# The fourth weight sum of every pair: made by VectorE in SBUF from a piece already there, and no longer in DRAM

## The chip, the core and the metric

The kernel runs on one core of one Trainium2 chip. TensorE (PE) multiplies matrices, and loads its weights through a stage of its own that the profile shows as PEld. VectorE (DVE), ScalarE (ACT) and GpSimd (POOL) do the element-wise work. SyncE (SP) issues DMAs; ACT and POOL issue some too. Each engine works through its own instructions in order, and semaphores hold it until what it needs is there. The metric is device time in microseconds (us), the median of several runs.

## What is computed

Two layers of an encoder trunk over 512 frames of width 1024, all in f32. What matters here is that the time goes into products of the activations with large weight matrices:

```python
for i in range(DEPTH):
    h = rmsnorm(x, norm1_g[i])
    z = h @ w_in[i] + b_in[i]
    ...
    merged = jax.nn.sigmoid(gm) * (y_m @ w_bm[i]) + jax.nn.sigmoid(gr) * (y_r @ w_br[i])
    x = x + merged @ w_out[i]
    h2 = rmsnorm(x, norm2_g[i])
    x = x + jnp.square(jax.nn.relu(h2 @ w_ff1[i] + b_ff1[i])) @ w_ff2[i] + b_ff2[i]
    h3 = rmsnorm(x, norm3_g[i])
    x = x + jax.nn.sigmoid(h3 @ w_pe_gate[i]) * (p[i] @ w_pe[i])
return rmsnorm(x, final_g)
```

## The kernel before

**Units.** The weights are used in an order that `unit_list` writes out: 165 units a layer, 330 in all. A "T8" unit is 1024 x 128 weights, 24 matmuls of 512 columns; "V" and "PE" units are of the same size. A "PAIR" unit is 1024 x 256 weights, computed by seven products instead of eight (Strassen's scheme in Winograd's form) of 12 matmuls of 256 columns each. There are 76 pairs.

**Each weight twice.** TensorE works on fp32r, so every weight piece is split into a high and a low half: `split` (lines 262 to 264) has ACT round it (`wh`) and DVE subtract (`wl`). Every product is then three matmuls: `wh` x high, `wh` x low, `wl` x high (lines 372 to 374 in a T8, 421 to 423 in a pair).

**The pieces of a pair.** The four blocks of a pair's weights are B11, B12, B21, B22, each 128 x 512 as stored. Seven products need seven weight operands: B11, B21, B22 and four sums, t1 = B12 + B11, t3 = B12 + B22, t2 = t1 + B22, t4 = t2 + B21 (the signs of the scheme are taken by the activations' side and by the readers of the products). They come in four pieces (`PIECE`): A = (B11, t1), B = (B21, t2), C = (B22, t3), each 128 x 1024, and D = (t4), 128 x 512.

**The sums.** They are made in DRAM while the kernel runs, a group of pairs at a time (20 groups; group g's tensors are `s{g}t1` to `s{g}t4`). Each sum takes two DMAs on POOL's queue (`step`, line 302): a copy of one block, then an accumulating copy of the other. `sum_steps` lists them: the first four steps of the next group alternate with the last four of this one. `due` gives the unit at which step k is issued, and `step` lets it wait for the last matmul emitted before that unit. There are 160 steps: steps 76 to 79, say, are t2 (copy of t1) of group 9, t1 of group 10, t2 (+= B22) of group 9, t3 of group 10.

**The weight feed.** `prep_next` prepares pieces in order: it lets `fill_raws` request loads ahead on SP's queue into the raw buffers `wr` (four, and a fifth, `wrx`, in the first part of a layer), then splits the next piece. A pair's A, B and C are two loads of 256 KB each, D is one. Split pieces lie in three buffers for A, B, C and T8 pieces, and one for D's. `ready` with `READY` says how far ahead of each product the pieces are prepared: before P7 of a pair, B of the next one.

**The order of a pair's products** (`run_pair`): P1, P5, then the P4 that the pair before had put off (`flush`), then P6, P2, P3, P7; its own P4 is put off in turn. P1, P6, P7 and P4 accumulate in one PSUM bank (suffix a), P5 and P3 in a second (c), P2 in a third (b). After each product, what stands in the bank is read (`done`): by DVE at L1209 or L1211 in the feed-forward pairs (`l0o10` is layer 0, block 1, pair 0), by ACT or DVE in the others (`pair_tiles`: L449 reads P2, L453 P3, L455 P7). The next product of the same bank may not begin before that.

**Other names in the steps.** `l1bgm` are the first gate tiles of layer 1, spilled to DRAM by ACT (`gm_spill`); `l1m0s` and `l1m0p` are the scores of the first mLSTM head and their weighted form (L648); `l?r0brk`, `l?r?o0` and `l?r?o1` are pairs of the retention heads; L542 is a POOL addition of the normalisation.

Of the kernel before, what the change touches and what calls it, by code (L numbers as in the profile page):

```python
# [38 lines left out]
OP = mybir.AluOpType  # L39
# [6 lines left out]
D = 1024  # L46
# [4 lines left out]
Q = 512  # L51
# [26 lines left out]
def ff_order():  # L78

    seq = [("f", 0, p) for p in range(4)]  # L80
    for b in range(3):
        seq.append(("f", b + 1, 0))
        seq += [("o", b, p) for p in range(4)]
        seq += [("f", b + 1, p) for p in range(1, 4)]
    return seq, [("o", 3, p) for p in range(4)]
# [3 lines left out]
PRODUCTS = {"P1": ("A", 0, 0), "P5": ("A", 1, 4), "P2": ("B", 0, 2), "P6": ("B", 1, 5), "P3": ("C", 0, 6),  # L89
            "P7": ("C", 1, 3), "P4": ("D", 0, 1)}  # L90

PIECE = {"A": ("B11", "t1"), "B": ("B21", "t2"), "C": ("B22", "t3"), "D": ("t4",)}

GIVEN = ("B11", "B12", "B21", "B22")
MADE = {"t1": ("B12", "B11"), "t3": ("B12", "B22"), "t2": ("t1", "B22"), "t4": ("t2", "B21")}

READY = {"P1": 2, "P4": 2, "P5": 3, "P2": 4, "P6": 4, "P3": 4, "P7": 5}


def due(k):  # L100

    return 3 + 5 * min(k, 20) // 4 + 7 * max(k - 20, 0) // 4


def groups():
# [108 lines left out]
def build(ctx, tc, ins, out):  # L214
    nc = tc.nc
    ve, ac, gp, te = nc.vector, nc.scalar, nc.gpsimd, nc.tensor
    units = [u for i in range(L) for u in unit_list(i)]
    NU = len(units)
# [43 lines left out]
    def split(src, hi_ap, lo_ap):  # L262
        a = ac.activation(hi_ap, src, AF.Copy)  # L263
        return a, ve.tensor_sub(lo_ap, src, hi_ap.bitcast(F32))  # L264

    def in_order(kind, *new):

        for a, b in zip(cur.get(kind, ()), new):
            tc.add_manual_dep(b.ins, a.ins.name, ORDER, reason="order of the weights")
        cur[kind] = new  # L270


    index, given, sums, k = {}, {}, {}, 0
    for g, v in groups().items():
        index[g] = len(index)
        for x in GIVEN:
            given[g, x] = ins["wpairs"][k:k + len(v)]
            k += len(v)
        for x in MADE:
            sums[g, x] = tc.dram_tile([len(v), P, Q], F32, name=f"s{index[g]}{x}")  # L280

    def block(g, x):
        return given[g, x] if x in GIVEN else sums[g, x]

    def flat(a):
        return a.rearrange("a p q -> (a p q)").rearrange("(r w) -> r w", r=P)

    def sum_steps():

        first = lambda g: [(g, "t1", 0), (g, "t3", 0), (g, "t1", 1), (g, "t3", 1)]  # L290
        second = lambda g: [(g, "t2", 0), (g, "t2", 1), (g, "t4", 0), (g, "t4", 1)]
        gs = list(index)
        out = first(gs[0])
        for a, b in zip(gs, gs[1:]):
            for x, y in zip(second(a), first(b)):
                out += [x, y]
        return out + second(gs[-1])

    steps = sum_steps()
    made = {g: 0 for g in index}  # L300

    def step():
# [3 lines left out]
        kw = {"accum_op": OP.add} if a else {}  # L306
        dma = gp.dma_start(flat(block(g, x)), flat(block(g, MADE[x][a])), max_dma_last_dim=4096, **kw)

        tc.add_manual_dep(dma.ins, cur["mm"].ins.name, SYNC, reason="pace of the sums")

    def next_unit():
        n = at["unit"]
        at["unit"] += 1
        while at["step"] < len(steps) and due(at["step"]) <= n:
            step()
        return n


    order = [(n, x) for n, u in enumerate(units) for x in (PIECE if u[0] == "PAIR" else (0,))]
    place = {x: k for k, x in enumerate(order)}  # L320
    raws, pieces = {}, {}

    room = unit_list(0).index(("T8", "w_out", 0, 0))
    cur["room"], cur["more"] = (), None
    at = {"unit": 0, "prep": 0, "load": 0, "whole": 0, "step": 0}

    def fill_raws(most=RAWS + 1):
        while at["load"] < len(order) and len(raws) < most:
            n, x = order[at["load"]]
            r = None  # L330
            if n in cur["room"] and cur["more"] not in raws:
                cur["more"] = n, x
                r = cur["low"].tile([P, UN], F32, name=f"wr{at['load']}", tag="wrx", bufs=1)
            elif len(raws) - (cur["more"] in raws) >= RAWS:
                break
            raws[n, x] = r = r or wpool.tile([P, UN], F32, name=f"wr{at['load']}", tag="wr", bufs=RAWS)
            if x:
                _, g, p = units[n]
                assert made[g] == 8, (g, made[g], at["unit"])
                for k, y in enumerate(PIECE[x]):  # L340
                    in_order("load", nc.sync.dma_start(r[:, k * Q:(k + 1) * Q], block(g, y)[p]))
            else:
                in_order("load", nc.sync.dma_start(r, ins["wstream"][at["whole"]]))
                at["whole"] += 1
            at["load"] += 1

    def prep_next():
        n, x = order[at["prep"]]
        at["prep"] += 1
        fill_raws()  # L350

        w = Q if x == "D" else UN
        pl = cur["last"] if n >= NU - LAST else wpool
        kw = {"tag": "d", "bufs": 2} if x == "D" else {"tag": "l", "bufs": 2 * LAST} if pl is not wpool else {
            "tag": "w", "bufs": 2 * PIECES}
        out_ = [pl.tile([P, w], F32R, name=f"w{a}{n}_{x}", **kw) for a in "hl"]
        r = raws.pop((n, x))
        in_order("prep", *split(r[:, :w], *out_))
        pieces[n, x] = out_

    def ready(k):
        while at["prep"] < min(len(order), k + 1):
            prep_next()
# [38 lines left out]
    def run_pair(name, act, done):  # L402
# [5 lines left out]
        def product(x):  # L408
            w, half, j = PRODUCTS[x]
            ready(place[n, "A"] + READY[x])  # L410
            wh, wl = [a[:, half * Q:(half + 1) * Q] for a in pieces[n, w]]
            b = {"P2": "b", "P5": "c", "P3": "c"}.get(x, "a")
            first = x in ("P1", "P2", "P5")
            if first:
                bank[b] = ps(f"{name}{b}")
            o = bank[b][:, 0:S]
            for k in range(4):
                s = slice(k * P, (k + 1) * P)
                h, l = act[k](j)
                f, e = first and k == 0, k == 3  # L420
                te.matmul(o, wh[:, s], h, start=f, stop=False, skip_group_check=True)
                te.matmul(o, wh[:, s], l, start=False, stop=False, skip_group_check=True)
                cur["mm"] = te.matmul(o, wl[:, s], h, start=False, stop=e, skip_group_check=True)
            done(x, o)

        def last():
            product("P4")
            for w in PIECE:
                del pieces[n, w]
# [338 lines left out]
    def big(name, dt):  # L768

        return [bpool.tile([P, T], dt, name=f"{name}{k}", tag="big", bufs=KT) for k in range(KT)]  # L770

    x = big("x0", F32)
# [6 lines left out]
    for _ in range(WARM):  # L779
        te.matmul(warm[:, 0:P], ones, ones, start=True, stop=True)  # L780
    fill_raws(1)
    for k in range(KT):
        nc.sync.dma_start(x[k], ins["xT"][k])
# [6 lines left out]
    for i in range(L):  # L790
# [228 lines left out]
        for d in range(4):  # L1019
# [8 lines left out]
            a = (f"l{i}m0{d}", 8 * (d // 2) + d % 2, qk[2 * (d // 2)][d % 2], qk[2 * (d // 2) + 1][d % 2], d < 2, n1)  # L1028
# [123 lines left out]
        if i == L - 1:  # L1152
            x_pool = phase("x", act_side)
            whole = x_pool.tile([P, KT, T], F32, name=f"l{i}x", tag="x")
            x = [whole[:, c, :] for c in range(KT)]
        else:
            x = big(f"l{i}x", F32)
# [78 lines left out]
        first, rest = ff_order()  # L1236
# [104 lines left out]
    cur["last"].release()  # L1341
    n3_pool.release()
    x_pool.release()
    assert at["unit"] == NU and at["prep"] == len(order) and not pieces and not raws and at["load"] == len(order) and at["step"] == len(steps)

# [110 lines left out]
```

## Time and profile before

| | us |
|---|---|
| three runs | 2367.16, 2362.84, 2363.36 |
| median | 2363.36 |
| the profiled execution: its span, first to last instruction (no other time of it is given) | 2361.2 |
| TensorE at full clock, mean over the span | 0.997 |
| split on ACT of the A, B, C pieces of pairs, one | 1.06 |
| split on DVE of the same, one | 1.22 |
| split of a D piece, ACT and DVE, one | 0.63 and 0.69 |
| steps of the sums on POOL's queue, issue to landing (lowest, median, highest) | 3.4, 8.2, 14.0 |
| loads of pair pieces on SP's queue, issue to landing (lowest, median, highest) | 2.5, 3.9, 10.7 |

The profile is one execution. Its views give, for each group of instructions, its line, engine, operation, output and inputs by name, shape and count, then busy time, mean duration of one in ns, idle time of the engine just before, and what ended most of that. A timeline row is start, duration, engine, line, operation, names, shape, count, and in brackets the idle time before it with what ended it. A row of waits is who waited, for whom, total us, times, longest.

### The profile page before, as it was taken

The numbers are of one execution on the slowest core, as the hardware profiler recorded it, in microseconds if no ns is written. First come the engines' busy times: TensorE is split into PE (matmuls) and PEld (weight loads), VectorE is DVE, ScalarE is ACT, GpSimd is POOL, SyncE is SP. The second block draws the span as 40 slices with busy tenths as digits, with TensorE's granted clock in tenths as the row PEclk, the third lists the DMA queues.
The fourth block names the chain that finished last, engine by engine and source line by source line (L and its number), as shares of the span: only waits on it lengthen the run. The fifth ranks groups of instructions, "written<-read, shape, count | busy, mean of one in ns | idle before, by whom it ended". The sixth has DMA issues, their size and how long they took to land. (4 is left out here: it accounts for less than half of the span.)

```text
span 2361.2 us, 35588 instructions
## 1 busy us (share of the span) xinstructions
PE 2339.5 (99%) x13788; PEld 2074.1 (88%) x13788; DVE 1579.5 (67%) x2435; ACT 1194.3 (51%) x1736; POOL 262.1 (11%) x380
## 2 busy tenths in 40 slices
PE   9999999999999999999999999999999999999998
PEld 7888898998998898899888888999989988998997
DVE  6877566764665676667778675676737656676675
ACT  5755344553553545445457563444526445455454
POOL 4121100000001100001321111000000020000012
PEclk9999999999999999999999999999999999999999
DMA  7766876768688777777776668776786894543441
GB/s 243 196 187 183 232 240 193 206 191 243 190 263 278 213 232 209 216 227 196 201 212 169 191 179 235 233 197 200 189 253 186 274 265 118 166 140 118 154 153 53
DMA packets 177576, 473.49 MB, mean 201 GB/s; under 512 B 17520, under 2 KB 19952, under 8 KB 177408
## 3 DMA queue, kind: packets, MB, share of 16 engines
q1 hardware_dynamic: 118512, 280.25, 35.3%
q0 software_dynamic: 41472, 159.39, 29.1%
q10 hardware_dynamic: 17424, 31.59, 3.7%
q8 instruction: 108, 1.77, 0.3%
q14 instruction: 60, 0.49, 0.1%
HBM read 456.48 MB, written 174.06 MB: 267 GB/s over the span
## 5 line engine op out<-in xcount | busy, mean ns | idle before, releaser
L263 ACT ACTIVATE wh<-wr 128x1024 fp32r<-128x1024 f32 x254 | 268.1, 1057 | 386.7 <-issue 55.2
L264 DVE TENSOR_TENSOR wl<-wr,wh 128x1024 fp32r<-128x1024 f32 x254 | 311.1, 1225 | 148.0 <-ACT wh L263 143.1
L263 ACT ACTIVATE wh_C<-wr 128x1024 fp32r<-128x1024 f32 x76 | 80.5, 1059 | 132.6 <-PE l0bm L373 13.1
L263 ACT ACTIVATE wh_B<-wr 128x1024 fp32r<-128x1024 f32 x76 | 80.4, 1058 | 85.3 <-PE l1bm L373 5.8
L264 DVE TENSOR_TENSOR wl_B<-wr,wh_B 128x1024 fp32r<-128x1024 f32 x76 | 93.9, 1235 | 43.7 <-ACT wh_B L263 43.2
L263 ACT ACTIVATE wh_A<-wr 128x1024 fp32r<-128x1024 f32 x76 | 80.1, 1055 | 76.6 <-PE l1f L373 11.3
L264 DVE TENSOR_TENSOR wl_A<-wr,wh_A 128x1024 fp32r<-128x1024 f32 x76 | 92.9, 1222 | 32.6 <-ACT wh_A L263 31.1
L264 DVE TENSOR_TENSOR wl_C<-wr,wh_C 128x1024 fp32r<-128x1024 f32 x76 | 92.8, 1221 | 29.0 <-ACT wh_C L263 29.0
L372 PE MATMUL l1f<-l1n2h,wh 128*128 128x512 f32 x256 | 99.8, 390 | 0.0
L372 PE MATMUL l0f<-l0n2h,wh 128*128 128x512 f32 x256 | 99.8, 390 | 0.0
L374 PE MATMUL l0f<-l0n2h,wl 128*128 128x512 f32 x256 | 99.7, 389 | 0.0
L374 PE MATMUL l1f<-l1n2h,wl 128*128 128x512 f32 x256 | 99.6, 389 | 0.0
L373 PE MATMUL l1f<-l1n2l,wh 128*128 128x512 f32 x256 | 99.6, 389 | 0.0
L373 PE MATMUL l0f<-l0n2l,wh 128*128 128x512 f32 x256 | 99.6, 389 | 0.0
L263 ACT ACTIVATE wh_D<-wr 128x512 fp32r<-128x512 f32 x76 | 47.6, 627 | 86.0 <-issue 5.3
L264 DVE TENSOR_TENSOR wl_D<-wr,wh_D 128x512 fp32r<-128x512 f32 x76 | 52.1, 686 | 46.3 <-ACT wh_D L263 43.9
L374 PEld LDWEIGHTS l1f<-l1n2h,wl 128*128 128x128 f32 x256 | 48.1, 188 | 10.1
L374 PEld LDWEIGHTS l0f<-l0n2h,wl 128*128 128x128 f32 x256 | 48.0, 188 | 10.0
L373 PEld LDWEIGHTS l0f<-l0n2l,wh 128*128 128x128 f32 x256 | 48.1, 188 | 9.8
L373 PEld LDWEIGHTS l1f<-l1n2l,wh 128*128 128x128 f32 x256 | 48.1, 188 | 9.8
L372 PEld LDWEIGHTS l0f<-l0n2h,wh 128*128 128x128 f32 x256 | 48.1, 188 | 9.8
L372 PEld LDWEIGHTS l1f<-l1n2h,wh 128*128 128x128 f32 x256 | 48.1, 188 | 9.8
(5492 smaller groups left out, 8236.2 us busy)
## 6 DMA issues: line engine op xcount, KB each, us to landing
wr<-wstream SPq DMA_DIRECT2D x254, 512.0 KB, 4.8
wr<-wpairs SPq DMA_DIRECT2D x228, 256.0 KB, 3.7
s0t<-wpairs POOLq DMA_DIRECT2D x6, 1024.0 KB, 8.2
s2t<-wpairs POOLq DMA_DIRECT2D x6, 1024.0 KB, 9.3
s3t<-wpairs POOLq DMA_DIRECT2D x6, 1024.0 KB, 9.0
s4t<-wpairs POOLq DMA_DIRECT2D x6, 1024.0 KB, 9.4
s5t<-wpairs POOLq DMA_DIRECT2D x6, 1024.0 KB, 9.7
s6t<-wpairs POOLq DMA_DIRECT2D x6, 1024.0 KB, 9.0
```

Of the source, the lines that this page charges most:

```text
L263: a = ac.activation(hi_ap, src, AF.Copy)
L264: return a, ve.tensor_sub(lo_ap, src, hi_ap.bitcast(F32))
L372: te.matmul(o, sh, mh, start=first, stop=False)
L373: te.matmul(o, sh, ml, start=False, stop=False)
L374: cur["mm"] = te.matmul(o, sl, mh, start=False, stop=last)
```

## The change

The DRAM sums lose t4: `MADE` has t1, t3 and t2, a group takes six steps, 120 in all. Piece D loses its load. When piece B = (B21, t2) has been split, DVE adds the second half of its raw buffer to the first, in place, which is t4; the buffer is kept under D's name until D is split from it. The list of steps now puts two of the next group's first steps behind each of this group's two last ones, and `due` spreads the 120 over about as many units as the 160 before: 7/4 of a unit a step for the first 15, then 9/4 (before: 5/4 for the first 20, then 7/4).

```diff
-PIECE = {"A": ("B11", "t1"), "B": ("B21", "t2"), "C": ("B22", "t3"), "D": ("t4",)}
+PIECE = {"A": ("B11", "t1"), "B": ("B21", "t2"), "C": ("B22", "t3"), "D": ()}
...
-MADE = {"t1": ("B12", "B11"), "t3": ("B12", "B22"), "t2": ("t1", "B22"), "t4": ("t2", "B21")}
+MADE = {"t1": ("B12", "B11"), "t3": ("B12", "B22"), "t2": ("t1", "B22")}
...
-    return 3 + 5 * min(k, 20) // 4 + 7 * max(k - 20, 0) // 4
+    return 3 + 7 * min(k, 15) // 4 + 9 * max(k - 15, 0) // 4
...
-        second = lambda g: [(g, "t2", 0), (g, "t2", 1), (g, "t4", 0), (g, "t4", 1)]
+        second = lambda g: [(g, "t2", 0), (g, "t2", 1)]
...
-            for x, y in zip(second(a), first(b)):
-                out += [x, y]
+            f = first(b)
+            for n, x in enumerate(second(a)):
+                out += [x] + f[2 * n:2 * n + 2]
...
+    loads = [(n, x) for n, x in order if x != "D"]
...
-        while at["load"] < len(order) and len(raws) < most:
-            n, x = order[at["load"]]
+        while at["load"] < len(loads) and len(raws) < most:
+            n, x = loads[at["load"]]
...
-                assert made[g] == 8, (g, made[g], at["unit"])
+                assert made[g] == 6, (g, made[g], at["unit"])
...
-        r = raws.pop((n, x))
+        r = raws.pop((n, "B" if x == "D" else x))
         in_order("prep", *split(r[:, :w], *out_))
         pieces[n, x] = out_
+        if x == "B":
+
+            ve.tensor_tensor(r[:, :Q], r[:, :Q], r[:, Q:], OP.add)
+            raws[n, x] = r
```

More of the change, by code (lines that the diff above doesn't have):

```diff
@@ L1343, in build @@
     x_pool.release()
-    assert at["unit"] == NU and at["prep"] == len(order) and not pieces and not raws and at["load"] == len(order) and at["step"] == len(steps)
+    assert at["unit"] == NU and at["prep"] == len(order) and not pieces and not raws and at["load"] == len(loads) and at["step"] == len(steps)
 def _pack_units(a):
```

## The prediction

> **What bounds the kernel now.** I read the page's engine shares first, then the waits of TensorE and of its weight loads, then the granted clock around the longest wait.
>
> ```profile
> span 2361.2 us, 35588 instructions
> PE 2339.5 (99%) x13788; PEld 2074.1 (88%) x13788; DVE 1579.5 (67%) x2435; ACT 1194.3 (51%) x1736; POOL 262.1 (11%) x380
> ```
> ```profile
> PE l1bgm L374 <- DVE wl L264: 2.0, 1, 2.0
> PE l0o33a L421 <- DVE l0x L1211: 1.6, 1, 1.6
> PE l1o33a L421 <- DVE l1x L1211: 1.6, 1, 1.6
> PE l0o11a L421 <- DVE l0x L1211: 1.5, 1, 1.5
> ...
> PE l0m0vp L625 <- DVE wl L264: 1.2, 1, 1.2
> ```
> ```profile
> 1283.90:1288.50 4.60, 4.60 (x13) 0.63 0.66 191
> ```
>
> TensorE is busy 2339.5 of 2361.2 us, so it sets the end; 21.7 us are idle, some of that before its first operands and in the closing normalisation. The waits inside the span are five, from 1.2 to 2.0 us. The third view is a window: length, PE busy, granted clock, DMA share, GB/s. After the longest wait the clock averages 0.63 for 4.6 us, which is another 4.6 x 0.37 = 1.7 us. No engine but TensorE can be relieved with any direct effect: the change can only remove or add waits of TensorE.
>
> **What two of these waits come from.** Both start with a transfer that is late because a 1 MB step of the weight sums is in flight. The next two views list issues, with KB and us from issue to landing: first around 922 and 924 us (unit 129, the first product of the second feed-forward block of layer 0), then the same kind of load at 2021 us, when no step runs, then a spill at 1246 us.
>
> ```profile
> s9t<-wpairs POOLq DMA_DIRECT2D x1, 1024.0 KB, 8.9
> ```
> ```profile
> wr<-s7t SPq DMA_DIRECT2D x1, 256.0 KB, 8.9
> ```
> ```profile
> wr<-s16t SPq DMA_DIRECT2D x1, 256.0 KB, 2.9
> ```
> ```profile
> gm_spill<-l1bgm1g ACTq DMA_DIRECT2D x1, 256.0 KB, 11.4
> ```
> ```profile
> 1235.68 0.55 POOL L307 DMA_DIRECT2D s12t<-s12t  x1 [11.47 <-PE l1bgm L374]
> 1245.61 0.92 POOL L307 DMA_DIRECT2D s13t<-wpairs  x1 [9.38 <-PE l1m0s L374]
> ```
> ```profile
> 933.53 1.06 ACT L263 ACTIVATE wh_C<-wr 128x1024 fp32r<-128x1024 f32 x1 [3.98 <-PE l0o11c L423]
> ```
> ```profile
> 1258.00 0.42 DVE L648 TENSOR_TENSOR l1m0p<-l1m0s,l1m0D 128x256 f32<-128x256 f32 x1 [2.26 <-DMA gm_spill<-l1bgm1g]
> ```
>
> The C piece's load, issued at 924.5, lands 8.9 us later at 933.4, and ScalarE starts its half of the split at 933.53 (the row names a matmul as releaser, but the landing is 0.1 us before). VectorE sits behind that split with the P1 addition of the same pair, and P6 waits for it: the 1.5 us of l0o11a. The spill shares the queues with the step issued at 1245.61 and takes 11.4 us; VectorE loses 2.26 us waiting for its buffer and the debt comes out as the 2.0 us wait at 1283.9 plus the 1.7 us of clock.
>
> **What goes.** Per group two of the eight steps (t4 from t2, then B21 onto it): 40 of 160. The page's rows for one group:
>
> ```profile
> s2t<-wpairs POOLq DMA_DIRECT2D x6, 1024.0 KB, 9.3
> ...
> wr<-s2t SPq DMA_DIRECT2D x16, 256.0 KB, 5.8
> ...
> s2t<-s2t POOLq DMA_DIRECT2D x2, 1024.0 KB, 5.8
> ```
>
> So some 15 us of transfer per group go (5.8 and 9.3), 40 issues leave POOL's queue and 76 loads of 256 KB leave SP's (4 of the 16 of each group). None of it is time of TensorE by itself.
>
> The steps that stay also move. Counting the list with the new due rule: the step of group 9 that hit unit 129 (t2 += B22, entry 78, 28 + 7x58//4) becomes entry 61, due 29 + 9x46//4 = 132, and group 10's t3 copy lands on 130. In layer 1, group 13's t1 += B11 goes from unit 176 to 175, that is to the place of the row at 1235.68, 10 us before the spill; the next one (t3 += B22) is due at 177, one unit after 1245.61. The spill then meets no fresh step. The raw buffer is not tighter: D takes no load, so A and B of the next pair are requested one piece earlier in program order, and C as before. B's buffer is held until D is split, but no load is asked for in that place until then; in the first part of a layer, where a fifth raw buffer exists, four loads wait for D's split, which I price at nothing to 0.5 us each, and take nothing, since their order leaves three loaded pieces ahead of them.
>
> I take both waits as gone: -1.5 and -(2.0 + 1.7) = **-5.2 us**. Bounds: -5.2 if no moved step hits again; +3.7 if they stay and one more hit like the worst is made. The value is nearer the first because unit 132 is the last pair of its stretch and because most steps in pair stretches cost TensorE nothing in the list of waits.
>
> The Trainium skill's page "DMA: Bandwidth & Descriptors", in "Queues, rings and completion order", says that each DMA engine takes turns among its queues packet by packet, so a load would share with a step rather than queue behind it. The rows disagree in size: 2.9 us alone, 8.9 beside a step, where even sharing of the load's bytes would give about twice 2.9. By the rule the moved steps could hardly make a stall, and the sum would keep its -5.2.
>
> **What comes.** 76 additions of 128x512, both operands in the raw buffer. The nearest row is the same operation, in place, SBUF only:
>
> ```profile
> L1141 DVE TENSOR_TENSOR l1bml<-l1bml,l1brl 128x512 f32<-128x512 f32 x8 | 5.5, 684 | 0.0
> ```
>
> That is 52 us more for VectorE, 1579.5 to 1632, 69%. Instructions overlap by 0.08 us (a 1.23 starting at 2036.58 is followed at 2037.72), so in a full queue each addition pushes what follows by 0.60. In most pairs this vanishes:
>
> ```profile
> 2036.58 1.23 DVE L264 TENSOR_TENSOR wl_B<-wr,wh_B 128x1024 fp32r<-128x1024 f32 x1 [0.39 <-ACT wh_B L263]
> 2037.72 0.41 DVE L1211 TENSOR_TENSOR l1x<-l1x,l1o02c 128x256 f32<-128x256 f32 x1
> 2038.32 0.42 DVE L1211 TENSOR_TENSOR l1x<-l1x,l1o02a 128x256 f32<-128x256 f32 x1 [0.18 <-PE l1o02a L423]
> 2039.30 1.23 DVE L264 TENSOR_TENSOR wl_C<-wr,wh_C 128x1024 fp32r<-128x1024 f32 x1 [0.56 <-ACT wh_C L263]
> ```
>
> The addition goes behind wl_B; the idle 0.18 and 0.56 absorb it before wl_C is due. The wait it adds is ScalarE's: wh_D, behind which the next A piece queues, needs the addition. Here that ends by 2038.5, and wl_C at 2039.30 is still ahead of D in both queues, so nothing is late.
>
> But P7's reader stands in the same queue. Products P1, P6, P7 and P4 pile up in one bank, so P4 may not start before VectorE has read P7, and B of the next pair is split just then. The program puts the addition ahead of that reader. Where TensorE already waits for it, the push is paid:
>
> ```profile
> PEld l1o32a L421 <- DVE l1x L1211: 0.6, 1, 0.6
> ...
> PEld l0o32a L421 <- DVE l0x L1211: 0.3, 1, 0.3
> ...
> PEld l0r0o1a L421 <- DVE l0r0o1y L455: 0.2, 1, 0.2
> ...
> PEld l1r0o1a L421 <- DVE l1r0o1y L455: 0.2, 1, 0.2
> ```
> ```profile
> 2287.24 1.21 DVE L264 TENSOR_TENSOR wl_B<-wr,wh_B 128x1024 fp32r<-128x1024 f32 x1
> 2288.37 0.41 DVE L1211 TENSOR_TENSOR l1x<-l1x,l1o32a 128x256 f32<-128x256 f32 x1
> ```
> ```profile
> 1602.28 0.42 DVE L453 TENSOR_TENSOR l1r0o1y<-l1r0o1c,l1r0o1y 128x256 f32<-128x256 f32 x1
> 1602.98 0.42 DVE L455 TENSOR_TENSOR l1r0o1y<-l1r0o1a,l1r0o1y 128x256 f32<-128x256 f32 x1 [0.29 <-PE l1r0o1a L423]
> ```
> ```profile
> 1486.29 1.22 DVE L264 TENSOR_TENSOR wl_B<-wr,wh_B 128x1024 fp32r<-128x1024 f32 x1
> 1487.42 0.42 DVE L455 TENSOR_TENSOR l1r0brky<-l1r0brka,l1r0brky 128x256 f32<-128x256 f32 x1
> ```
> ```profile
> 1488.02 0.29 PE L421 MATMUL l1r0brka<-l1xnh,wh_D 128*128 128x256 f32 x1
> ```
>
> Three kinds of place. o32, once a layer: no idle between, 0.60 each, 1.2. The second gate pair of each retention head (8 rows alike, l0r0o1a the first and l1r0o1a the last): L453 may be followed from 1602.62, the reader starts at 1602.98, so 0.60 - 0.36 = 0.24 each, 1.9. r0brk, once a layer: the reader ends at 1487.84 and P4 starts at 1488.02; 0.06 of that is the hand-over seen elsewhere, so 0.12 is slack and 0.48 is paid, 1.0. Together **+4.1 us**. Bounds: 0 if the additions come out behind the readers; 12 x 0.69 = 8.3 if nothing absorbs them. I take 4.1, the rows' own spacing.
>
> ```profile
> 1118.85 1.31 POOL L542 TENSOR_TENSOR l0n3sum<-l0n3sum,l0n3sq 128x512 f32<-128x512 f32 x1 [1.61 <-ACT l0n3sq L534]
> ```
> ```profile
> 1119.05 2.20 DVE L264 TENSOR_TENSOR wl_B<-wr,wh_B 128x1024 fp32r<-128x1024 f32 x1
> ```
>
> A VectorE operation beside a POOL sum took 2.20 where its like takes 1.21. The Trainium skill's page "SBUF — State Buffer" says so as a rule that speaks against the change: a VectorE instruction with two SBUF inputs and a GpSimd one that reads SBUF lock each other out. By it each addition that meets a POOL sum costs up to 1.3 more. The rows keep them apart: the sum here ends at 1120.16, before wl_B does.
>
> **Sum.** The page gives a span of 2361.2 and nothing outside it; the median of the runs, 2363.4, is 2.2 above, and I carry that over. 2361.2 + 2.2 + 4.1 - 5.2 = 2362.3: **about 2362 us, no change** within 0.2% (4.7 us), which is about what a measurement of this kernel can tell.
>
> **Rivals.** *Slower: the moved steps hit again.* A step issued within some 2 us ahead of a C load (as at 922.4 and 924.5) or of a spill makes a new wait; unit 130 is the suspect in the stretch where 129 was. Then the additions stand uncompensated: 2363.4 + 4.1 = 2367.5, and with one more hit of 1.5 to 3.7, 2369 to 2371. For it: the steps that stay are as long as before. Against: a quarter fewer, and only two hits now in 160. Decided if two hits or more remain. Chance 0.29.
>
> *Faster: the additions cost nothing*, being placed behind the readers, and both hits go: 2363.4 - 5.2 = 2358.2, or less if a further wait falls. For it: VectorE is 33% idle. Against: program order. Chance 0.13.
>
> *Nothing moves*: waits stay and the additions are absorbed, 2363.4; it is inside the forecast's own result. Chance 0.08.
>
> Forecast: 0.50. Same is 0.58 with the third rival, slower 0.29, faster 0.13. The range 2358 to 2371 reaches from the faster rival to the slower one with a further hit; the forecast's own is 2360 to 2367.
>
> **What would show it.** Right: the waits at l0o11a and l1bgm gone from TensorE's list, no clock below 1.00 near 1284; weight-load waits at l?r?o1a up from 0.2 to about 0.45, at r0brk new with about 0.5, at o32 0.9 and 1.2; gm_spill landing under 6 us. Wrong: a new wait behind a landing, the additions not directly behind wl_B, or weight-load waits at P4 unchanged.

## The result and the profile after

| | before | after |
|---|---|---|
| median of 20 runs each, us | 2364.25 | 2360.11 |
| lowest and highest | 2359.0, 2368.8 | 2358.0, 2362.1 |
| the profiled execution, span | 2361.2 | 2359.5 |
| TensorE's waits, summed | 26.96 | 21.35 |

The ratio is 0.9979, interval 0.9972 to 0.9986: 4.1 us less by the medians, 0.2%. The last row is worked out from the trace: wherever a matmul starts more than 25 ns later behind the last one than the median for the same two shapes in the same kernel (118 ns between two of 256 columns, 227 ns between two of 512, and so on), the excess is added. By it one place can be compared from kernel to kernel, and "excess" below means that. One execution of before in the last batch below took 9146 us at a granted clock of 0.24 and is left out of every figure.

The page of the changed kernel, and the longest of TensorE's waits (who waited for whom, total us, times, longest):

```profile
span 2359.5 us, 35353 instructions
PE 2341.2 (99%) x13788; PEld 2077.1 (88%) x13788; DVE 1623.0 (69%) x2511; ACT 1194.0 (51%) x1736; POOL 232.2 (10%) x340
```
```profile
PE l0o33a L427 <- DVE l0x L1217: 2.0, 2, 1.5
PE l1o33a L427 <- DVE l1x L1217: 2.0, 2, 1.5
...
PE l0m0vp L631 <- DVE wl L264: 1.4, 1, 1.4
```

The two waits that the prediction priced at 1.5 and 2.0 us are not in the list. That at l?o33a (a ? stands for both layers) is now two waits in one row: the old one ahead of the put-off P4 (excess 1.67 and 1.65 us, before 1.81 and 1.77), and a new one ahead of P6 (0.68 and 0.64 us; before 0.08).

The additions as a group, and the spill (KB, us from issue to landing; 11.4 before):

```profile
L364 DVE TENSOR_TENSOR wr<-wr 128x512 f32<-128x512 f32 x76 | 52.0, 684 | 0.7
```
```profile
gm_spill<-l1bgm1g ACTq DMA_DIRECT2D x1, 256.0 KB, 3.9
```

76 additions of 684 ns, none longer than 693: the size of the term was right, and none overlapped with work of POOL.

The spans differ by 1.7 us where the waits differ by 5.6. A window over the same products of the first feed-forward block of layer 0, in before and after (length, PE busy and matmuls, clock, DMA share, GB/s), shows where most of that went:

```profile
862.00:872.00 10.00, 10.00 (x91) 1.00 0.92 288
```
```profile
862.00:872.00 10.00, 10.00 (x87) 1.00 0.76 232
```

At the same full clock before's matmuls follow each other faster here: their starts are 113.3 ns apart, after's 117.7. In the profile of before four of the eight feed-forward stretches (l0o0, l1o0, l1o1, l1o3) ran at the fast spacing for most of their length, in that of after and in the ten other profiles of this study none. This gave that one execution of before some 4.5 us (the starts of the same products, compared between the two traces, drift by +1.2 us in l0o0, +2.4 in l1o0 and l1o1 together, and +1.1 in l1o3). It is a property of the execution, as the next section shows, so one span against one span misleads, and the medians do not.

### The profile page after: what moved, and what is told of

It is laid out like the page before. It is cut to its first block, busy times and chain, and to the rows that moved or that the text cites. A ratio compares the mean times of both kernels' runs of the same rounds, so it can differ in the third digit from the quotient of the medians.

```text
span 2359.5 us, 35353 instructions
## 1 busy us (share of the span) xinstructions
PE 2341.2 (99%) x13788; PEld 2077.1 (88%) x13788; DVE 1623.0 (69%) x2511; ACT 1194.0 (51%) x1736; POOL 232.2 (10%) x340
## 3 DMA queue, kind: packets, MB, share of 16 engines
q8 instruction: 108, 1.77, 0.3%
## 5 line engine op out<-in xcount | busy, mean ns | idle before, releaser
L380 PEld LDWEIGHTS l1f<-l1n2h,wl 128*128 128x128 f32 x256 | 48.0, 188 | 10.2
```

The costliest lines, as they stand in the source:

```text
L380: cur["mm"] = te.matmul(o, sl, mh, start=False, stop=last)
```

## The experiments

The kernels were timed in three batches, each beside before on one chip; before's medians there were 2366.1 us (again, moved2, hits, oldslots), 2365.4 (noadd, pinned, late33, moved3) and 2366.3 (after_b, late33_b). Each batch had a chip of its own, so kernels of different batches are best compared by their ratios to before.

**The kernel before, again** (again).

> The kernel before, unchanged, for a second profile of it. Theory 'two steps': the waits at l0o11a (1.5 us) and at l1bgm (2.0 us, with the clock near 0.63 behind it) belong to the program and stand here again, within 0.3 us. Rival 'luck of an execution': they differ from run to run, and at least one is gone or under half. Beside that: in the profile of before the matmuls of 128x256 of four of the eight feed-forward stretches follow each other at 113.3 ns, those of the other four, and of all eight in the changed kernel, at 117.7 ns. If that belongs to the kernel, the same four are fast here; if it is set anew in each execution, others are. Time: 2364 us, ratio 1.000, by both.

Measured: 2364.99 us, ratio 0.9995 (0.9986 to 1.0004), span of its profile 2365.8. TensorE's waits in it:

```profile
PE l1bgm L374 <- DVE wl L264: 1.7, 1, 1.7
...
PE l1wo L372 <- ACT l1mh L263: 0.8, 1, 0.8
...
PE l0wo L372 <- ACT l0mh L263: 0.4, 1, 0.4
```

Each theory had half. l1bgm stays, so it belongs to the program; but 1.89 us of excess instead of 2.12 left the clock at 1.00 (the last section comes back to this). l0o11a is gone: the step was issued 2.1 us later and the C load took 7.4 us instead of 8.9. In its place stand waits at the output products, which the first profile does not have, and the summed excess is about the same, 27.44 us. None of the stretches is fast but a few tens of matmuls at pair joints. So before is not one number: which transfers collide, and the spacing of the matmuls, differ from one execution to the next.

**Two steps moved in the kernel before** (moved2).

> The kernel before with only two of its 160 steps moved: t2 += B22 of group 9 from unit 129 to 128, t1 += B11 of group 13 from unit 176 to 177. All four sums are still made in DRAM. Theory 'two steps': the waits at l0o11a and l1bgm go (under 0.3 us each, clock 1.00 near 1284), 5.2 us less, 2359 us, ratio 0.998. Rival 'order': the l1bgm wait went because the changed kernel has the split wl of unit 182 earlier in VectorE's order; here that order is as before, so the wait of about 2 us stays, and only l0o11a's 1.5 us goes, 2362.5 us, ratio 0.9993. Rival 'bytes': the gain comes with the smaller traffic, and nothing is gained here, ratio 1.000.

```diff
-    return 3 + 5 * min(k, 20) // 4 + 7 * max(k - 20, 0) // 4
+    moved = {78: 128, 105: 177}
+    return moved.get(k, 3 + 5 * min(k, 20) // 4 + 7 * max(k - 20, 0) // 4)
```

Measured: 2367.61 us, ratio 1.0003 (0.9994 to 1.0011). No theory had this. l0o11a is gone, but l1bgm is twice as long. Its row, then VectorE's and POOL's rows (start, duration, and in brackets the idle time before with what ended it), then the windows behind it:

```profile
PE l1bgm L375 <- DVE wl L265: 3.9, 1, 3.9
```
```profile
1263.50 0.29 DVE L649 TENSOR_TENSOR l1m0p<-l1m0s,l1m0D 128x128 f32<-128x128 f32 x1 [4.62 <-POOL l1m0D L888]
```
```profile
1262.23 0.93 POOL L308 DMA_DIRECT2D s12t<-wpairs  x1 [5.99 <-PE l1m1z L375]
1262.83 0.64 POOL L888 TENSOR_SCALAR_AFFINE_SELECT l1m0D<-l1m0D 128x128 f32<-128x128 f32 x1
```
```profile
1285.00:1290.00 5.00, 3.81 (x9) 0.50 0.45 125
```

The spill landed after 4.0 us, as theory 'two steps' wants. But the moved step pushed the next one (t4 of group 12) later, and that one stood in POOL's queue ahead of the last mask of the head (L888). The row names a matmul as what ended the step's wait, but the step was issued 0.31 us behind the landing of the one before it (1261.92), as it was in before (1258.84 behind 1258.53). The mask came after that, and VectorE stood idle for 4.62 us. A wait at l1wo (1.3 us) is here as well, as in again. The spill is one way to make VectorE idle here, POOL's queue is another, and TensorE pays for either 20 us later.

**Two steps put back in the changed kernel** (hits).

> The changed kernel with two of its 120 steps put back where the old ones stood: t3 copy of group 10 from unit 130 to 129, t1 += B11 of group 13 from unit 175 to 176. Nothing else differs, the order of the instructions on VectorE and TensorE neither. Theory 'two steps': a wait of about 1.5 us returns at l0o11a and one of 1.5 to 2 us at l1bgm with low clock behind it, gm_spill lands after 10 us or more; 2360.1 + 5.2 = 2365.3 us, ratio to before 1.000. Rival 'order': no wait at l1bgm above 0.3 us, at l0o11a perhaps; 2360 to 2362 us, ratio 0.998 to 0.999. Rival 'bytes': neither wait, 2360 us.

```diff
-    return 3 + 7 * min(k, 15) // 4 + 9 * max(k - 15, 0) // 4
+    moved = {60: 129, 80: 176}
+    return moved.get(k, 3 + 7 * min(k, 15) // 4 + 9 * max(k - 15, 0) // 4)
```

Measured: 2363.59 us, ratio 0.9987 (0.9979 to 0.9996).

```profile
PE l1bgm L381 <- DVE wl L265: 1.5, 1, 1.5
```
```profile
1256.70 0.56 DVE L655 TENSOR_TENSOR l1m0p<-l1m0s,l1m0D 128x384 f32<-128x384 f32 x1 [1.87 <-POOL l1m0D L894]
```
```profile
1255.45 0.90 POOL L309 DMA_DIRECT2D s13t<-wpairs  x1 [3.95 <-PE l1m1z L381]
1256.04 0.62 POOL L894 TENSOR_SCALAR_AFFINE_SELECT l1m0D<-l1m0D 128x128 f32<-128x128 f32 x1
```

The order of the instructions is that of the changed kernel, and the wait at l1bgm comes back (excess 1.71 us against 0.07), so here it is the step's place that made it and not VectorE's order. The spill takes 10.4 us again, but VectorE does not wait for it: it waits for a mask behind a step, which again was issued 0.31 us behind a landing (1255.14). The clock stays at 1.00, and no wait comes back at l0o11a, where this step is another copy than the one of before. 'Two steps' holds for l1bgm, with POOL's queue as the way; for l0o11a it is not shown.

**The removal without the re-timing** (oldslots).

> The changed kernel with the additions, but the 120 steps that are left stand at the units that they had before; the places of the 40 steps of t4 are left empty. This is the removal without the re-timing. Theory 'two steps': the steps at units 129 and 176 hit as before, so both waits are here, and the additions cost under 1 us: 2364 to 2365 us, ratio 1.000. Rival 'bytes': with a quarter of the steps gone the two that are left in place find the queues emptier, and the waits go: 2360 us, ratio 0.998.

```diff
-    return 3 + 7 * min(k, 15) // 4 + 9 * max(k - 15, 0) // 4
+    return 3 + 5 * min(k, 20) // 4 + 7 * max(k - 20, 0) // 4
...
-        second = lambda g: [(g, "t2", 0), (g, "t2", 1)]
+        second = lambda g: [(g, "t2", 0), (g, "t2", 1), (g, "t4", 0), (g, "t4", 1)]
...
         at["step"] += 1
+        if x == "t4":
+            return
```

(The list alternates as before.) Measured: 2363.28 us, ratio 0.9988 (0.9979 to 0.9997), between the two theories. One wait of the two is there, and none at l0wo or l1wo:

```profile
PE l0o11a L428 <- DVE l0x L1218: 1.0, 1, 1.0
```

So l0o11a is the step's at unit 129, beside the same C load (in again, with that step in place, the load came in time); and l1bgm goes (excess 0.19) though the step at 176 is still there and the spill still takes 10.2 us. The spill lands 9.2 us behind VectorE's first row on that head's masks instead of 10.4, VectorE waits 1.37 us for it instead of 2.26, and the t4 step that stood between the masks in before (1258.84) is gone. VectorE's order is another one too, and which of these takes the wait away is not shown. By these ratios (0.9988 against 0.9979 and 0.9976, all in different batches and each with an interval of about 0.0009 to either side) roughly half of the gain is the removal, the rest the new places; by the summed excess (26.96, 23.48, 21.35) it is 3.5 of 5.6 us.

**A rearrangement of five steps in the kernel before** (moved3).

> The kernel before with five of its 160 steps moved: the one of unit 129 to 128, and of those around the first mLSTM head of layer 1, units 175 and 176 to 174 and 175, 178 and 180 both to 181. So none is issued between the gate tiles' spill and the fourth mask on POOL's queue. Theory 'VectorE's debt': the l1bgm wait is the time in which VectorE stood idle between 1248 and 1264 us, because the spill landed late or because a mask stood behind a step in POOL's queue, ahead of 18 us without a gap; with both gone its idle falls from 6.0 us to about 2.6, and the wait from 1.7 to 2.0 us to under 0.3, clock 1.00, gm_spill lands under 5 us. Against moved2 (4.1 us) that is 4 us and its clock 2 us less; against the kernel before 2 to 3.7 us less, ratio 0.9985 to 0.999. Rival: the loads of the T8 pieces are what is late; then the wait stays above 1 us.

```diff
-    return 3 + 5 * min(k, 20) // 4 + 7 * max(k - 20, 0) // 4
+    moved = {78: 128, 104: 174, 105: 175, 106: 181, 107: 181}
+    return moved.get(k, 3 + 5 * min(k, 20) // 4 + 7 * max(k - 20, 0) // 4)
```

Measured: 2371.72 us, ratio 1.0024 (1.0015 to 1.0033): slower. The part at hand behaved: the spill took 4.0 us, and the wait at l1bgm fell, though to 0.7 and not under 0.3. One of 1.0 us came ahead of it (l1m1z, at 1245 us), and a worse one a few us behind it:

```profile
PE l1m0ot L682 <- DVE l1m0num L676: 3.8, 1, 3.8
...
PE l1bgm L375 <- DVE wl L265: 0.7, 1, 0.7
```
```profile
1288.73 0.92 POOL L308 DMA_DIRECT2D s13t<-wpairs  x1 [8.20 <-DVE l1xnl L265]
1289.31 0.56 POOL L907 TENSOR_TENSOR l1m0hv<-l1m0mv,l1m0q 128x4 f32<-128x4 f32 x1
```

Two steps due at one unit follow each other on POOL; the second was issued 9 us behind the first, when that had landed (1288.42), and l1m0hv, a tiny POOL operation on which VectorE and then TensorE depend, sat behind it.

VectorE's busy time in the 17 us from its first row on that head's masks, in before, again, moved2, hits, oldslots, moved3 and after in this order (length, busy and instructions, clock, DMA share, GB/s):

```profile
1247.55:1264.55 17.00, 10.97 (x20) 1.00 0.90 213
```
```profile
1247.92:1264.92 17.00, 11.23 (x20) 1.00 0.92 222
```
```profile
1247.89:1264.89 17.00, 9.01 (x17) 1.00 0.80 210
```
```profile
1248.60:1265.60 17.00, 12.54 (x23) 1.00 1.02 284
```
```profile
1248.76:1265.76 17.00, 12.74 (x24) 1.00 0.69 200
```
```profile
1249.80:1266.80 17.00, 13.60 (x25) 1.00 0.42 138
```
```profile
1248.89:1265.89 17.00, 14.41 (x26) 1.00 0.90 255
```

Where VectorE's order is the same but for one swap at most, its loss is paid one for one. From again to moved2: 2.22 us less busy, excess at l1bgm 1.89 to 4.10. From after to hits: 1.87 less, 0.07 to 1.71. Between kernels of different order the rule does not hold: hits has 12.54 us busy and 1.71 of excess, oldslots 12.74 and 0.19. So VectorE's order has a part in this wait too, and no run here separates it.

**No additions** (noadd).

> The changed kernel without the 76 additions: piece D is split from B21 alone, so P4's products are computed from another operand; all else stays. It measures what the additions cost. The prediction's term: +4.1 us, so 2360.1 - 4.1 = 2356.0 us here. Theory 'the order absorbs them': the build puts the additions behind the reader of P7, or fills TensorE's wait with transposes, wherever it would show; only the P6 of the last feed-forward pair of each layer waits longer (0.68 and 0.64 us in the changed kernel), so 1 us goes, about 2359 us. In the profile then: no wait above 0.1 us at P6 of l0o33a and l1o33a, weight-load waits at l?r?o1a at 0.2 as with the additions.

```diff
-            ve.tensor_tensor(r[:, :Q], r[:, :Q], r[:, Q:], OP.add)
```

Measured: 2358.99 us, ratio 0.9968 (0.9955 to 0.9980); the changed kernel had 2360.11 in its own runs and 2360.50 in the third batch (ratios 0.9979 and 0.9976). The waits ahead of P6 at l?o33a are gone, those ahead of P4 at l?r?o1a as with the additions. The additions cost 1.1 to 1.5 us by these medians, 1.2 by the two waits ahead of P6, and not 4.1.

**TensorE's order held** (pinned).

> The changed kernel with TensorE's order at the second gate pair of each retention head held as in the kernel before: the transposes of the head's second tile but the first stay behind P4, instead of two of them being put ahead of it. VectorE's order is nearly the same. Theory 'the order absorbs them': each addition does push the reader of P7 by the 0.24 us that the prediction reckons, and two transposes of 0.12 us hide it; with them gone the wait ahead of P4 at l?r?o1a rises from 0.13 us to about 0.37 in all eight places, 8 x 0.24 = 1.9 us more, 2362.0 us. Rival 'no push': VectorE's reader is not late at all, the wait stays at 0.13, 2360.1 us.

```diff
-            te.transpose(o[:, j * P:(j + 1) * P], num[:, j, v * P:(v + 1) * P], ident)
+            t = te.transpose(o[:, j * P:(j + 1) * P], num[:, j, v * P:(v + 1) * P], ident)
+            if "r" in nm and v * NT + j > NT:
+                tc.add_manual_dep(t.ins, cur["mm"].ins.name, ORDER, reason="behind P4")
```

Measured: 2363.14 us, ratio 0.9988 (0.9979 to 0.9997). The weight loads' waits in after and in this kernel, one row of the eight alike, and VectorE's and TensorE's rows of after at that place:

```profile
PEld l0r1o1a L427 <- DVE l0r1o1y L461: 0.2, 1, 0.2
```
```profile
PEld l0r0o1a L427 <- DVE l0r0o1y L461: 0.4, 1, 0.4
```
```profile
1597.96 0.41 DVE L459 TENSOR_TENSOR l1r0o1y<-l1r0o1c,l1r0o1y 128x256 f32<-128x256 f32 x1
1598.29 0.68 DVE L364 TENSOR_TENSOR wr<-wr 128x512 f32<-128x512 f32 x1
1598.89 0.41 DVE L461 TENSOR_TENSOR l1r0o1y<-l1r0o1a,l1r0o1y 128x256 f32<-128x256 f32 x1
```
```profile
1598.47 0.93 PE L687 MATMUL l1r0ot<-ident,l1r0num 128*128 128x128 f32 x7
1599.36 0.38 PE L427 MATMUL l1r0o1a<-l1xnh,wh_D 128*128 128x256 f32 x1
```

The addition does stand between the readers of P3 and P7, and the reader of P7 starts 0.93 us behind that of P3 (before 0.70): the push of 0.24 us is there. But TensorE has seven transposes ahead of P4 where before had five, and 2 x 0.11 us of other work fills the push. With the order held, the excess ahead of P4 rises from 0.13 to 0.35 us in all eight places, 8 x 0.22 = 1.8 us: the prediction's term to a tenth. (The median lies 2.6 to 3.0 us above those of the changed kernel in other batches. The profile accounts for 1.8 here and 0.7 among the first matmuls of that execution; whether the latter is the kernel's is open.)

**Two additions moved** (late33, then after_b and late33_b).

> The changed kernel with two of the 76 additions, those of the last feed-forward pair of each layer, moved behind the reader of that pair's P1. Theory: the new waits of 0.68 and 0.64 us at l0o33a and l1o33a come from the addition that stands ahead of wl_C and that reader; they fall under 0.1 us, the waits ahead of the put-off P4 grow back by 0.1 each, about 1.1 us gained, 2359.0 us. Rival: they come from wl_C or the normalisation beside it; the waits stay, 2360.1 us.

```diff
+        if x == "D" and units[n][1][1:] == ("ff3",) and units[n][2] == 3:
+            t = ve.tensor_tensor(r[:, :Q], r[:, :Q], r[:, Q:], OP.add)
+            tc.add_manual_dep(t.ins, cur["read"].ins.name, ORDER, reason="behind the reader of P1")
...
-            ve.tensor_tensor(r[:, :Q], r[:, :Q], r[:, Q:], OP.add)
+            if units[n][1][1:] != ("ff3",) or units[n][2] != 3:
+                ve.tensor_tensor(r[:, :Q], r[:, :Q], r[:, Q:], OP.add)
...
-                    ve.tensor_tensor(y, y, o, op)
+                    cur["read"] = ve.tensor_tensor(y, y, o, op)
```

Measured: 2358.86 us, ratio 0.9967 (0.9954 to 0.9979), as fast as without any addition. The waits ahead of P6 are gone; those ahead of the put-off P4 did not grow by 0.1 us each as expected (excess 1.53 and 1.54 against 1.67 and 1.65). Then beside the changed kernel in one batch:

> The changed kernel again, on the chip of the next run: a second profile of it, and its time beside that of the version with two additions moved. By the first profile: P6 of l0o33a and l1o33a wait 0.68 and 0.64 us, no wait at l1bgm, l0wo, l1wo above 0.2 us; ratio to before 0.997 to 0.998.

> The version with the two additions of the last feed-forward pairs behind the reader of P1, again: if the gain over the changed kernel is real it is 1 to 1.3 us less than the run before it on the same chip, with the two waits at P6 gone; if it was the chip, the two agree within 0.5 us.

Measured: 2360.50 us, ratio 0.9976 (0.9966 to 0.9986), and 2358.86 us, ratio 0.9968 (0.9955 to 0.9980): 1.6 us apart by the medians, 1.3 by the spans (2358.5 and 2357.2) and 1.0 by the summed excess (20.61 and 19.56). VectorE at the last pair of layer 1, in the changed kernel's first profile and in this version:

```profile
2285.94 1.21 DVE L264 TENSOR_TENSOR wl_B<-wr,wh_B 128x1024 fp32r<-128x1024 f32 x1
2287.07 0.41 DVE L1217 TENSOR_TENSOR l1x<-l1x,l1o32a 128x256 f32<-128x256 f32 x1
2287.40 0.68 DVE L364 TENSOR_TENSOR wr<-wr 128x512 f32<-128x512 f32 x1
2288.01 1.21 DVE L264 TENSOR_TENSOR wl_C<-wr,wh_C 128x1024 fp32r<-128x1024 f32 x1
2289.14 0.41 DVE L1217 TENSOR_TENSOR l1x<-l1x,l1o33a 128x256 f32<-128x256 f32 x1
```
```profile
2285.59 1.21 DVE L264 TENSOR_TENSOR wl_C<-wr,wh_C 128x1024 fp32r<-128x1024 f32 x1
2286.73 0.41 DVE L1220 TENSOR_TENSOR l1x<-l1x,l1o33a 128x256 f32<-128x256 f32 x1
2287.06 0.68 DVE L361 TENSOR_TENSOR wr<-wr 128x512 f32<-128x512 f32 x1
```

In the changed kernel the addition comes behind the reader of P7 (l1o32a), so o32 pays nothing, but ahead of wl_C and of the reader of P1 (l1o33a), for which P6 waits. Behind that reader it costs nothing. This version is the fastest of all that were run.

## Why the prediction held, and where not

The forecast was no change, 2362 us, with 2358 to 2371; it came out at 2360.1, a gain of 0.2%, at the edge of what it called no change. The sum was -5.2 + 4.1, a gain of 1.1 us. With the terms as measured it is -5.3 + 1.1 to 1.5, a gain of 3.8 to 4.2, and 4.1 was measured: one of the two terms was wrong by some 3 us, and only the width of "no change" kept the forecast inside it. Two of the signs that it had set for being wrong came up: 20 of the 76 additions stand directly behind wl_B and 56 do not, and the weight-load waits at P4 are not higher (0.2 at l?r?o1a). Step by step:

- **"I take both waits as gone: -5.2".** Held in size: in the first pair of profiles l0o11a gives 1.66 us of excess and l1bgm 2.05, and the half clock behind it 1.6. But it is no constant of the two kernels: in the second profile of before l0o11a is absent, the clock stays at 1.00, and waits at the output products stand in its place. That the term fits to 0.1 us is luck.
- **"The spill shares the queues with the step" as the cause of l1bgm.** Half of it. Where VectorE's order is the same, its idle time sets the wait, and the spill is one of its sources. That a step stands in POOL's queue ahead of the masks, and holds them while it waits for TensorE or for the step before, is the other; I put no price on that queue. How much of the wait went with the changed order of VectorE is not shown.
- **"Some 15 us of transfer per group go ... none of it is time of TensorE by itself".** Too low at zero: with the old places kept, the removal already gave roughly half of the gain.
- **"What comes", +4.1: the step that failed.** Measured 1.1 to 1.5. The duration (0.684 us) and the push (0.24 at the retention heads) were right. What was wrong is "the program puts the addition ahead of that reader", and the price that followed. Each engine's order is set when the kernel is built and it changed with the addition: at o32 and r0brk the addition stands behind the reader of P7 (0 instead of 1.2 and 1.0), and at the eight retention pairs two transposes moved ahead of P4 (0 instead of 1.9). And P6 of the last pair, whose reader stands behind wl_C in a queue without a gap, was not on my list: 0.60 and 0.56 us there are nearly all that the additions cost.
- **"The raw buffer is not tighter".** Nothing in the waits speaks against it.
- **The rivals.** The faster one described the additions best, and with -5.2 its 2358.2 is 1.9 from the time; it got 0.13 because I took the program's order for the engine's. 'The moved steps hit again' did not happen in this change, but hits, moved2 and moved3 show that it is easily made.
- **"Some 2.2 us above the span".** The profiled execution of before was itself a lucky one by some 4.5 us of fast matmuls, and had the stall at l0o11a. The second profile of before has neither, its span is 2365.8, and the gain by medians is larger than the gain by first spans.

The waits at l0m3a and l1m3a (0.28 us each) went as well, through another order of three matmuls, and a new one of 0.4 stands at l1m2z (0.14 in the second profile of the changed kernel): small changes that no step of the prediction had.

## What to carry to other kernels

Ask what stands behind each issue of a DMA in an engine's queue, not only what its bytes share: an engine that issues paced transfers and also makes a small operand can hold the operand back. A queue without gaps ahead of the bounding engine paid each idle microsecond back one for one here, 20 us later, so look for the loss where the debt is made and not where it shows. Before an added instruction is priced by its place in the program, look whether the order of the engines is the program's: here the other engines' orders moved to cover it, and two additions put elsewhere by hand gave the rest back.

## What was not expected of the hardware

The 128x256 matmuls of the feed-forward pairs run in two rhythms at the same granted clock of 1.00: starts 113.3 ns apart or 117.7, with the weight load 110 or 115 ns ahead of its matmul. In the first profile of before the fast one begins at 847.0 us, right behind a gap of 223 ns after the first matmul of a P7 (l0o00), and lasts to the end of the stretch; a gap of 222 ns at 929.2 us, in l0o10, did not start it. A whole stretch (four pairs of 84 matmuls) would differ by 1.5 us. What starts it stays open; no kernel of this study was made to do so.

The clock fell to half behind some waits and not behind others: after excesses of 1.71 to 1.89 us it stayed at 1.00 (l1bgm in hits and again, l0o33a in before), after 2.01 (l1o33a in again), 2.12, 3.99 and 4.10 it fell. The length alone does not decide it. In every trace here the granted clock changes only at times that lie whole multiples of 3.413 us apart: in before it is 0.50 from 1284.89 to 1288.30 us and next changes at 2349.84, which is 1 and 311 such stretches. What went with a fall was how little TensorE had been busy in one such stretch. The rows below are before's wait at l1bgm and the stretch behind it, and then, in again, the stretch with most of the wait at l1bgm, after which the clock stayed, and the one with the wait at l1o33a, after which it fell (length, PE busy and matmuls, clock, DMA share, GB/s):

```profile
1281.48:1284.89 3.41, 1.45 (x6) 1.00 0.00 0
1284.89:1288.30 3.41, 3.41 (x9) 0.50 0.83 234
```
```profile
1282.28:1285.69 3.41, 1.69 (x7) 1.00 0.21 40
...
2299.46:2302.87 3.41, 1.57 (x9) 1.00 0.25 101
2302.87:2306.28 3.41, 3.41 (x15) 0.50 0.74 220
```

Up to 2340 us, in all twelve traces, the four stretches with 1.57 us of busy time or less are followed by one at half clock, which costs up to another 1.7 us, and none of those with 1.69 us or more at full clock is. In the closing normalisation one with 1.82 us is (again, from 2350.66 us), so the busy time of the profile is not the whole rule. That a wait of 2 us across two stretches would cost only its length is not shown; no run here has one. Behind the waits of 3.99 and 4.10 us two stretches ran at half clock. The Trainium skill's page "TensorE: Matmul & The Clock Gate", "What's actually happening", puts the clock at half after an idle window of about 3.4 us; the rows here show it behind waits of 2.0 to 2.1 us, in stretches that were busy for up to 1.57 of 3.41 us, and here the rows decide.
